# One core, a gMLP and RWKV-7 encoder: the inverse's stores on GpSimd's queue with another order of loads and post-processing, and the low parts of three weight matrices kept in DRAM

## The chip, the cores and the metric

The kernel runs on one core of one Trainium2 chip. The metric is the time of one execution on the device in microseconds. Engines are TensorE (PE; PEld is its loading of weights), VectorE (DVE), ScalarE (ACT), GpSimd (POOL) and SyncE (SP). SP, ACT and POOL can issue DMAs; "SPq", "ACTq" and "POOLq" in the profile are such issues.

## What is computed

An encoder trunk for 1024 tokens of 1024 features, with two residual layers, a SwiGLU FFN after each and a final RMSNorm:

```python
for layer in range(DEPTH):                      # DEPTH = 2
    hn = rms_norm(h, mix_norm[layer])
    if layer % 2 == 0:
        h = h + hybrid_ab_mixer(hn, ...)        # gMLP + pooled means
    else:
        y, v_first = rwkv7_time_mix(hn, ...)
        h = h + y
    h = h + swiglu(rms_norm(h, ffn_norm[layer]), w_gate, w_up, w_down)
return rms_norm(h, final_norm)
```

In the RWKV layer, with xx the shift by one token,

```python
xr, xw, xk, xv, xa, xg = [h + xx * mu[i] for i in range(6)]
r, k, v = xr @ w_r, xk @ w_k, xv @ w_v
# per head, for each token t:
sa = einsum('bhvk,bhk->bhv', state, a_t)
state = state * w_t[:, :, None, :] + sa[..., None] * b_t[:, :, None, :] + v_t[..., None] * k_t[:, :, None, :]
y_t = einsum('bhvk,bhk->bhv', state, r_t)
# then a normalisation per head, a bonus, a gate and @ w_o
```

## The kernel before

**Tiles and halves.** The tokens are worked on in two halves of 512 (h = 0 and 1). Features are 8 tiles of 128. Dense products are float32 by three float32r products: a weight tile of 128x1024 is split into a high part (ACT copies it, L159, "whi", "dhi", "ahi") and a low part (DVE subtracts the high part from the raw tile, L160, "wlo", "dlo", "alo"), and `mm3` (L407 to L411) adds hi·hi, lo·hi and hi·lo.

**Weights.** All weight tiles stand in one list, `plan`, in the order of their use. `load_at` (L123) loads a raw tile by a DMA of ACT's queue, `split_at` splits it, and `take` hands a tile out and keeps two loads and one split ahead. The pool `wst` holds 3 buffers each of raw, high and low tiles.

**Order.** The program is written as generators that are interleaved: `drive(dense, side)` mixes a stream of dense matmuls with side work. A scheduler then orders the instructions of each engine by dependences, priorities and its own estimates; on the chip each engine works through its list in that order, and an instruction that waits holds up all behind it on the same engine.

**Stages.** By the trace: the mixer of layer 0 until about 420 us; its FFN up to 560; the down projection of half 0 from 560 to 740 (`steps_a`, with `wa1` beside it); gates and low-rank factors until 830; `project(0)` from 830 to 1045; `recur(0)` from 1045 to 1250; output projection and norms until 1380; `project(1)` to 1590, `recur(1)` to 1810; the rest of the FFN and the final norm to the end.

**`project(h)`** computes for each pair of heads p = 0 to 7 the products for k and r (weights "k" and "r"), the decays (`cum`, a scan on DVE, L1347), and from them `ar` and `bk`, the scaled operands of the recurrence. Of these, `ar`'s first column (L1374) and the product kkn·av (L1377) are on POOL; L1381 on DVE makes `bk` from the latter, and `late` lets PE multiply `ar` and `bk` (L1257, tile "aux"). SP stores ar and bk to `ab_d`. After p = 3 and p = 7 starts `invert` (L1432 to L1454): 31 steps of two DVE operations (L1443, L1448) invert unit lower triangular 32x32 blocks of four pairs, a copy (L1450) transposes, and three DMAs of SP store the result in `xi_d` (L1452: 64 partitions of 32 rows of 64 numbers; L1454 twice: 64 of 32 rows of 32). These steps lie between the other DVE work: the first inversion beside p = 4 to 7, the second beside the products for v.

**`recur(h)`** works through 8 chunks of 64 tokens. `load(c)` loads ab (L1506), XT (two DMAs from `xi_d`, L1510) and uv (L1513, L1514) by SP. For each chunk come `gram` (bk times ar, then masked into gt, L1530), `flip_bk` (products with the identity), `below` (products with XT) and `burst` (the chain through the state S, uv and the output ysb). All of these matmuls have one line, L1491. Dense matmuls of the FFN are put in between. `stream` (L1842) loads h for them. After two chunks, `post` normalises their output (statistics per head, L1690), in pieces that `between` calls during the next burst; `turn_out` (L1714) transposes and gates it.

Of the kernel before, what the change touches and what calls it, by code (L numbers as in the profile page):

```python
# [16 lines left out]
P = 128  # L17
D = 1024
# [27 lines left out]
def tile_trunk(  # L46
# [79 lines left out]
    def whl():  # L126
        return wst.tile([P, D], F32R, tag="whi", name="whi"), wst.tile([P, D], F32R, tag="wlo", name="wlo")

    def split_at(i):
        if i >= len(plan) or i in ready:  # L130
            return
        load_at(i)
        if i not in raws:
            return
        key, _, view, dest = plan[i]
        if key[0] in makes:
            ready[i] = makes[key[0]](i)
            return
        raw = raws[i]
        to = (dest or whl)()  # L140
        if to is None:
            return
        hi, lo = to
        splits.get(key[0], lambda i, *t: split(*t))(key[1], view(raw), view(hi), view(lo))
        ready[i] = hi, lo

    def take(key):
        i = pos[0]
        assert plan[i][0] == key, (plan[i][0], key)
        pos[0] += 1  # L150
        split_at(i)
        load_at(i + 1)
        if i + 1 in raws:
            load_at(i + 2)
        split_at(i + 1)
        return ready.pop(i)

# [1274 lines left out]
    def invert(h, p0, iat, tmp):  # L1432
# [18 lines left out]
        to = xi_d[h][p0 : p0 + 4].rearrange("p r c q i x -> (p r c) q i x")  # L1451
        sp.dma_start(to[:, 0, :, 0:64], x2[0:64].rearrange("s i a j -> s i (a j)"))  # L1452
        for q in range(2):
            sp.dma_start(to[:, q, :, 64 - 32 * q : 96 - 32 * q], x2[64:128, :, 0, :])  # L1454

# [13 lines left out]
    def recur(h, wp, stream, ratio):  # L1469
# [34 lines left out]
        def load(c):  # L1504
            ab = wt("ar", 2, [P, 2, 8, 2, 64])
            sp.dma_start(ab, ab_d[h][c])  # L1506
            ar, bk = ab[:, 0], ab[:, 1]
            XT = wt("XT", 2, [P, 8, 96])
            for r in range(2):
                sp.dma_start(XT[rows[r]], xi_d[h][:, r ^ (c % 2), c].rearrange("p q i x -> (q i) p x"))  # L1510
            uv = wt("uv", 2, [P, 2, 8, 64])
            vs = v_d[h][c * 64 : c * 64 + 64]
            sp.dma_start(uv[64:128, 0], vs[:, 0])  # L1513
            loaded[0] = sp.dma_start(uv[0:64, 1], vs[:, 1])  # L1514
            gt = wt("gt", 2, [P, 8, 2, P])
            C[c] = (ar, bk, uv, gt, XT)

# [71 lines left out]
        def burst(c, bkt, w1):  # L1589
# [53 lines left out]
            if more:  # L1643
                bkt = flip_bk(c + 1)
                if turned or pieces:
                    for _ in pieces.pop():
                        pass
                    turned.pop()()
# [14 lines left out]

        turned, chain, pieces = [], [None], []

        def between():
            if pieces:
                with tc.issue_after(chain[0]):
                    next(pieces[0], None)

        def post(jj):
            ysb = [ypair.pop(0) for _ in range(2)]
            j = h * 4 + jj
# [13 lines left out]
            yield  # L1687
            for r in range(2):
                for p in range(8):
                    dve.bn_stats(out=st[:, r, p, :], in_=ysb[r][:, p, :])  # L1690
                yield
# [49 lines left out]
        with tc.issue_after(loaded[0].ins):  # L1741
            stream_loaded = stream()
        with tc.issue_after(stream_loaded):
            load(1)
        yield START * ratio
# [8 lines left out]
        for c in range(8):  # L1754
            bkt, w1 = yield from burst(c, bkt, w1)
            yield BURST / 2
            if c % 2 == 1:
                pieces[:] = [post(c // 2)]
                next(pieces[0])
            yield BURST / 2  # L1760
        for _ in pieces[0]:
# [198 lines left out]

    drive(steps_a, wa1())
    hn1 = project_norm(0, np_, norm_bcast(acc[0]))
# [148 lines left out]
```

## Time and profile before

| | us |
|---|---|
| runs | 2401.15, 2406.74, 2410.41 (median 2406.74) |
| profiled execution, device time | 2407.23 |
| its span in the trace | 2405.5 |
| PE busy | 2319.2 |
| DVE busy | 1464.6 |
| ACT busy | 946.9 |
| POOL busy | 171.2 |
| DMA traffic | 347.97 MB, mean 145 GB/s |

The profiled execution is 0.5 us longer than the median of the runs. Its span leaves out 1.7 us around it. A busy time sums the instructions of an engine; "PEclk" is the share of the full TensorE clock that was granted; "DMA share" is the mean busy share of 16 DMA engines. A row of waits gives the waiting engine, tile and line, then what ended the wait, the total, the number of times and the longest. Line numbers are those of the kernel before.

### The profile page before, as it was taken

The page shows a single profiled execution, that of the slowest core. Times are in us where ns is not written, and L with a number is a line of the kernel's source. Part 1 is how long each engine was busy: PE and PEld are TensorE (multiplying, and loading weights), DVE is VectorE, ACT ScalarE, POOL GpSimd, SP SyncE. Part 2 cuts the span into 40 slices and gives each one's busy share as a digit, 9 for nine tenths or more (in the row PEclk, how much of TensorE's full clock was granted, in tenths as well). Part 3 has the DMA queues.
Part 4 walks back from the last instruction along what each step waited for, and adds up shares of the span by engine and source line. Part 5 has one row for each costly group of instructions (what it writes and reads, how often), then busy time and mean ns, then how long its engine had stood idle before and what let it go on. Part 6 is the DMA issues. An engine that isn't in the chain of part 4 may idle for free.

```text
span 2405.5 us, 37578 instructions
## 1 busy us (share of the span) xinstructions
PE 2319.2 (96%) x15315; PEld 1893.9 (79%) x15315; DVE 1464.6 (61%) x2312; ACT 946.9 (39%) x1467; POOL 171.2 (7%) x195
## 2 busy tenths in 40 slices
PE   8999999999999999889899999998999999999998
PEld 6888888888888788667777777777778788888886
DVE  6445775665568858656768958765664546444443
ACT  6233444444224755323336665423332225222223
POOL 0200000000000022101100022101010001000001
PEclk9999999999999999999999999999999999999999
DMA  5114472334765565775445475776534433433231
GB/s 181 53 49 145 149 198 83 129 99 146 283 226 191 156 173 140 209 218 157 130 135 165 148 199 147 193 222 177 163 89 149 123 88 119 127 96 97 79 114 44
DMA packets 446157, 347.97 MB, mean 145 GB/s; under 512 B 119776, under 2 KB 393312, under 8 KB 443680
## 3 DMA queue, kind: packets, MB, share of 16 engines
q10 hardware_dynamic: 266048, 195.33, 27.3%
q1 hardware_dynamic: 179936, 150.25, 20.9%
q8 instruction: 120, 1.97, 0.4%
q14 instruction: 53, 0.43, 0.1%
HBM read 266.47 MB, written 79.04 MB: 144 GB/s over the span
## 4 chain that ended last, share of the span: by engine, by line
PE 77%; DVE 9%; DMA 6%; issue 2%; ACT 2%; SPq 2%; POOL 2%; ACTq 0%; POOLq 0%; DVEq 0%
PE mm L409 17%; PE mm L410 17%; PE mm L411 17%; PE mm L740 5%; PE mm L742 5%; PE mm L741 5%; PE sm L1491 3%; DMA ar<-ab_d 1%; DVE wlo L160 1%; DMA raw<-y_d 1%; SPq L1454 1%; DVE it L1443 1%; DMA raw<-in_ffn_w_down_dram 1%; PE mm L590 1%; PE mm L591 1%
## 5 line engine op out<-in xcount | busy, mean ns | idle before, releaser
L409 PE MATMUL mm<-ahi,whi 128*128 128x512 f32 x1376 | 541.0, 394 | 4.2 <-ACT ahi L159 2.6
L410 PE MATMUL mm<-alo,whi 128*128 128x512 f32 x1376 | 542.0, 394 | 0.9 <-DVE alo L160 0.9
L411 PE MATMUL mm<-ahi,wlo 128*128 128x512 f32 x1376 | 540.6, 393 | 1.6 <-DVE wlo L160 1.6
L159 ACT ACTIVATE whi<-raw 128x1024 fp32r<-128x1024 f32 (+2 forms) x284 | 286.3, 1014 | 507.1 <-PE mm L410 367.7
L160 DVE TENSOR_TENSOR wlo<-raw,whi 128x1024 fp32r<-128x1024 f32 (+2 forms) x284 | 337.6, 1192 | 233.6 <-ACT whi L159 212.4
L409 PEld LDWEIGHTS mm<-ahi,whi 128*128 128x128 f32 x1376 | 259.0, 188 | 62.9 <-issue 3.5
L411 PEld LDWEIGHTS mm<-ahi,wlo 128*128 128x128 f32 x1376 | 259.2, 188 | 58.5 <-DVE wlo L160 2.9
L410 PEld LDWEIGHTS mm<-alo,whi 128*128 128x128 f32 x1376 | 259.3, 188 | 57.4 <-issue 2.9
L503 DVE TENSOR_TENSOR h<-h,mm 128x512 f32<-128x512 f32 x276 | 185.9, 684 | 156.1 <-PE mm L411 152.9
L411 PE MATMUL mm<-hidhi,wdlo 128*128 128x512 f32 x304 | 119.6, 394 | 0.0
L409 PE MATMUL mm<-hidhi,wdhi 128*128 128x512 f32 x304 | 117.2, 392 | 2.3 <-ACT sg L957 2.3
L410 PE MATMUL mm<-hidlo,wdhi 128*128 128x512 f32 x304 | 118.6, 390 | 0.0
L740 PE MATMUL mm<-ahi,whi 128*128 128x512 f32 x296 | 115.6, 390 | 0.0
L741 PE MATMUL mm<-alo,whi 128*128 128x512 f32 x296 | 115.2, 389 | 0.0
L742 PE MATMUL mm<-ahi,wlo 128*128 128x512 f32 x296 | 113.6, 389 | 0.0
L965 DVE TENSOR_TENSOR sg<-sg,mm 128x512 f32<-128x512 f32 x52 | 35.7, 686 | 125.7 <-PE mm L411 125.7
L159 ACT ACTIVATE wdhi<-raw 128x1024 fp32r<-128x1024 f32 x42 | 43.6, 1058 | 169.0 <-PE mm L410 126.9
L160 DVE TENSOR_TENSOR wdlo<-raw,wdhi 128x1024 fp32r<-128x1024 f32 x42 | 51.4, 1223 | 30.9 <-ACT wdhi L159 29.2
L409 PEld LDWEIGHTS mm<-hidhi,wdhi 128*128 128x128 f32 x304 | 57.2, 188 | 14.7 <-ACT sg L957 2.7
L411 PEld LDWEIGHTS mm<-hidhi,wdlo 128*128 128x128 f32 x304 | 57.2, 188 | 12.2 <-issue 0.5
L410 PEld LDWEIGHTS mm<-hidlo,wdhi 128*128 128x128 f32 x304 | 57.2, 188 | 12.0 <-issue 0.2
L409 PE MATMUL mm<-xhi,whi 128*128 128x512 f32 (+1 forms) x160 | 64.9, 406 | 0.0
(392 smaller groups left out, 4226.2 us busy)
## 6 DMA issues: line engine op xcount, KB each, us to landing
raw<-in_ffn_w_down_dram ACTq DMA_DIRECT2D x88, 512.0 KB
raw<-in_ffn_w_gate_dram ACTq DMA_DIRECT2D x74, 512.0 KB
raw<-in_ffn_w_up_dram ACTq DMA_DIRECT2D x74, 512.0 KB
hid_d<-hid SPq DMA_DIRECT2D x36, 512.0 KB
ar<-ab_d SPq DMA_DIRECT2D x16, 1024.0 KB
hd<-hid_d SPq DMA_DIRECT2D x26, 512.0 KB
raw<-in_ab_w_in_dram ACTq DMA_DIRECT2D x16, 512.0 KB
raw<-in_ab_w_out_dram ACTq DMA_DIRECT2D x16, 512.0 KB
```

Of the source, the lines that this page charges most:

```text
L159: act.activation(hi, src, AF.Copy)
L160: (eng or dve).tensor_tensor(out=lo, in0=src, in1=hi.bitcast(F32), op=ALU.subtract)
L409: pe.matmul(o, whi, xhi, start=first, stop=False)
L410: pe.matmul(o, whi, xlo, start=False, stop=False)
L411: newest[0] = pe.matmul(o, wlo, xhi, start=False, stop=last).ins
L503: dve.tensor_tensor(out=H[h][:, m, :], in0=H[h][:, m, :], in1=o, op=ALU.add)
L590: pe.matmul(ops[j], xhi[:, k, sl], whi[:, kk], start=(k == 0), stop=False)
L740: pe.matmul(o, wh[:, k, :], x[0][:, k, :], start=st, stop=False, skip_group_check=True)
L741: pe.matmul(o, wh[:, k, :], x[1][:, k, :], start=False, stop=False, skip_group_check=True)
L742: pe.matmul(o, wl[:, k, :], x[0][:, k, :], start=False, stop=k == 3, skip_group_check=True)
L965: dve.tensor_tensor(out=s, in0=s, in1=o, op=ALU.mult)
L1491: i = f(*args, **kw)
```

## The change

It has two parts.

**Part A, the recurrence's data.** `invert` issues its three stores from GpSimd's queue. `load(c)` loads ab and uv first and XT after them, in a new function `load_x`; for chunk 0, XT is loaded behind the four loads of `stream`, and chunk 1 behind that. The post-processing of two chunks starts ahead of the odd chunk's burst instead of behind it: one piece is let through in an odd burst, any number in an even one, and the output is taken from the list piece by piece.

**Part B, the low parts.** `prepare` runs beside the down projection of half 0, behind `wa1`. For w_r and w_k it works through four units of 1 MB each: a DMA of GpSimd loads the unit, ACT copies the high part and DVE subtracts it (two operations each), and a DMA of GpSimd stores the low part in `rk_d`. In both projections, the low tiles of r and k are loaded from there by SP, two tiles ahead, and only the high part is made. The low tiles of v are made in half 0 as before and stored by SP in `vl_d`, and loaded from there in half 1.

```diff
+    rk_d = dram.tile([2, 4, P, 8, 256], F32, name="rk_d")
+    vl_d = dram.tile([8, P, 8, P], F32, name="vl_d")
+    lows = {}
...
+    def low_at(i):
+        if i >= len(plan) or i in lows:
+            return
+        key = plan[i][0]
+        if low_of(key) is not None and (key[0] != "v" or key[1]):
+            lows[i] = wst.tile([P, D], F32R, tag="wlo", name="wlo")
+            sp.dma_start(v3(lows[i].bitcast(F32)), low_of(key))
...
     def split_at(i):
...
         raw = raws[i]
+        low_at(i)
+        if i in lows:
+            ready[i] = wst.tile([P, D], F32R, tag="whi", name="whi"), lows[i]
+            act.activation(ready[i][0], raw, AF.Copy)
+            return
...
         ready[i] = hi, lo
+        if low_of(key) is not None:
+            sp.dma_start(low_of(key), v3(lo.bitcast(F32)))
...
         dve.tensor_copy(x2[:, :, 0, :], xi.rearrange("p i c -> p c i"))
         to = xi_d[h][p0 : p0 + 4].rearrange("p r c q i x -> (p r c) q i x")
-        sp.dma_start(to[:, 0, :, 0:64], x2[0:64].rearrange("s i a j -> s i (a j)"))
+        pool.dma_start(to[:, 0, :, 0:64], x2[0:64].rearrange("s i a j -> s i (a j)"))
         for q in range(2):
-            sp.dma_start(to[:, q, :, 64 - 32 * q : 96 - 32 * q], x2[64:128, :, 0, :])
+            pool.dma_start(to[:, q, :, 64 - 32 * q : 96 - 32 * q], x2[64:128, :, 0, :])
...
-            XT = wt("XT", 2, [P, 8, 96])
-            for r in range(2):
-                sp.dma_start(XT[rows[r]], xi_d[h][:, r ^ (c % 2), c].rearrange("p q i x -> (q i) p x"))
...
+            if c:
+                load_x(c)
+
+        def load_x(c):
+            for r in range(2):
+                loaded[0] = sp.dma_start(C[c][4][rows[r]], xi_d[h][:, r ^ (c % 2), c].rearrange("p q i x -> (q i) p x"))
...
         with tc.issue_after(stream_loaded):
+            load_x(0)
+        with tc.issue_after(loaded[0].ins):
             load(1)
...
         for c in range(8):
-            bkt, w1 = yield from burst(c, bkt, w1)
-            yield BURST / 2
             if c % 2 == 1:
                 pieces[:] = [post(c // 2)]
                 next(pieces[0])
-            yield BURST / 2
+            open_[0] = (99, 1)[c % 2]
+            bkt, w1 = yield from burst(c, bkt, w1)
+            yield BURST
...
+    def prepare():
+        yield from wa1()
+        for n, w in enumerate((rwkv_w_r[0], rwkv_w_k[0])):
+            for u in range(4):
+                raw, hi = (pr.tile([P, 8, 256], t, tag=g, bufs=2, name=g) for t, g in ((F32, "praw"), (F32R, "phi")))
+                pool.dma_start(raw, w[:, u * 256 : u * 256 + 256].rearrange("(k p) m -> p k m", p=P))
+                for q in (slice(0, 4), slice(4, 8)):
+                    yield 0.8
+                    tc.cur_priority += AHEAD
+                    act.activation(hi[:, q], raw[:, q], AF.Copy)
+                    dve.tensor_tensor(
+                        out=raw[:, q].bitcast(F32R), in0=raw[:, q], in1=hi[:, q].bitcast(F32), op=ALU.subtract
+                    )
+                    tc.cur_priority -= AHEAD
+                pool.dma_start(rk_d[n, u], raw)
...
-    drive(steps_a, wa1())
+    drive(steps_a, prepare())
```

Counted over the program, DVE's subtractions for wlo fall from 254 to 214, and 16 for praw come in; ACT gets 16 copies phi; GpSimd 8 loads and 8 stores of 1 MB and the 12 stores of the inverse; SP 32 loads from rk_d, 8 stores to and 8 loads from vl_d, and loses the 12. The matmuls are the same in number.

The lines of the changed kernel differ: L1374, L1377 and L1437 of before are L1402, L1405 and L1465; L1381 is L1409; L1452 and L1454 are L1480 and L1482; L1425 is L1453; L1506, L1510, L1513 and L1514 are L1534, L1546, L1538 and L1539.

**SP at the start of `recur(1)`.** Before:

```order
L1425 DMA v_d_1977<-epx 256x1x256
L1452 DMA xi_d_1983<-xi 64x32x64
L1454 DMA xi_d_1983<-xi 64x32x32 x2
L1506 DMA ar<-ab_d_1975 128x2048
L1510 DMA XT<-xi_d_1983 64x8x96 x2
L1513 DMA uv<-v_d_1977 64x512
L1514 DMA uv<-v_d_1977 64x512
L1740 DMA S<-state_d 128x512
L1842 DMA h<-h_d_85 128x1024 x4
L1506 DMA ar<-ab_d_1975 128x2048
```

Now:

```order
L1453 DMA v_d_1979<-epx 256x1x256
L1534 DMA ar<-ab_d_1977 128x2048
L1538 DMA uv<-v_d_1979 64x512
L1539 DMA uv<-v_d_1979 64x512
L1771 DMA S<-state_d 128x512
L1875 DMA h<-h_d_87 128x1024 x4
L1546 DMA XT<-xi_d_1985 64x8x96 x2
L1534 DMA ar<-ab_d_1977 128x2048
```

The inverse's stores are gone from SP, the ab load (ar) follows the last store of v, and the load of XT stands behind the loads of h. In `recur(0)` the order is the same, without the load of S.

**GpSimd at p = 7 of `project(0)`.** The names are ar (L1374), kkn (L1377), the exponentials' copy pct and the cleared tile xi of the second inversion. Before:

```order
L1081 TENSOR_SCALAR sg<-sg 128x512
L1081 TENSOR_SCALAR av<-av 128x512
L1353 COPY pct<-epx 128x8
L1374 TENSOR_SCALAR ar<-kkn 128x8
L1377 TENSOR_TENSOR kkn<-kkn,av 128x512
L1437 MEMSET xi 128x2048
```

Now:

```order
L1109 TENSOR_SCALAR sg<-sg 128x512
L1109 TENSOR_SCALAR av<-av 128x512
L1381 COPY pct<-epx 128x8
L1402 TENSOR_SCALAR ar<-kkn 128x8
L1480 DMA xi_d_1984<-xi 64x32x64
L1482 DMA xi_d_1984<-xi 64x32x32 x2
L1405 TENSOR_TENSOR kkn<-kkn,av 128x512
L1465 MEMSET xi 128x2048
```

The first inversion's three stores stand between ar and kkn. In `project(1)` they stand two rows higher, between av and pct.

**DVE from p = 6 to the end of the first inversion of `project(0)`.** it and xi are the inversion's steps, the copy of xi its end, bk (L1381, now L1409) what PE waits for. Before, around bk of p = 7:

```order
L1448 TENSOR_TENSOR xi<-xi,it 128x7x25
L160 TENSOR_TENSOR alo<-raw,ahi 128x1024
L1182 TENSOR_TENSOR xlo<-mix,xhi 128x512
L1189 SCALAR_TENSOR_TENSOR mix<-hn_5530,vec,mix 128x512
L1443 TENSOR_TENSOR it<-iat,xi 128x156
L1381 TENSOR_TENSOR bk<-kkn,em 128x8x64
```

Now, from the last steps of the inversion:

```order
L1476 TENSOR_TENSOR xi<-xi,it 128x31
L188 TENSOR_TENSOR wlo<-raw,whi 128x1024
L1478 COPY xi<-xi 128x32x32
L1210 TENSOR_TENSOR xlo<-mix,xhi 128x512
L188 TENSOR_TENSOR alo<-raw,ahi 128x1024
L1398 SCALAR_TENSOR_TENSOR ar<-kkn,epx 128x8x63
L1210 TENSOR_TENSOR xlo<-mix,xhi 128x512
L1217 SCALAR_TENSOR_TENSOR mix<-hn_5600,vec,mix 128x512 x2
L188 TENSOR_TENSOR alo<-raw,ahi 128x1024
L1210 TENSOR_TENSOR xlo<-mix,xhi 128x512 x2
L1409 TENSOR_TENSOR bk<-kkn,em 128x8x64
```

Before, bk of p = 7 came with six steps of the inversion still to do; now the inversion and its copy are done ahead of it.

More of the change, by code (lines that the diff above doesn't have):

```diff
@@ L127, in whl, with low_of @@
         return wst.tile([P, D], F32R, tag="whi", name="whi"), wst.tile([P, D], F32R, tag="wlo", name="wlo")
+    rk_d = dram.tile([2, 4, P, 8, 256], F32, name="rk_d")
+    vl_d = dram.tile([8, P, 8, P], F32, name="vl_d")
+    lows = {}
+    def low_of(key):
+        if key[0] in ("r", "k"):
+            return rk_d["rk".index(key[0]), key[2] // 2][:, :, key[2] % 2 * P : key[2] % 2 * P + P]
+        return vl_d[key[2] * 4 + key[3]] if key[0] == "v" else None
+    def low_at(i):
[5 more added lines that the diff above has]
+            sp.dma_start(v3(lows[i].bitcast(F32)), low_of(key))
     def split_at(i):
@@ L155, in take @@
         split_at(i + 1)
+        i2 = i + 2
+        if i2 < len(plan) and plan[i2][0][0] in acts:
+            i2 += 1
+        low_at(i2)
         return ready.pop(i)
@@ L1514, in load @@
             loaded[0] = sp.dma_start(uv[0:64, 1], vs[:, 1])
-            gt = wt("gt", 2, [P, 8, 2, P])
-            C[c] = (ar, bk, uv, gt, XT)
+            C[c] = (ar, bk, uv, wt("gt", 2, [P, 8, 2, P]), wt("XT", 2, [P, 8, 96]))
+            if c:
[3 more added lines that the diff above has]
+                loaded[0] = sp.dma_start(C[c][4][rows[r]], xi_d[h][:, r ^ (c % 2), c].rearrange("p q i x -> (q i) p x"))
         def gram(c, q):
@@ L1644, in burst @@
                 bkt = flip_bk(c + 1)
-                if turned or pieces:
-                    for _ in pieces.pop():
-                        pass
+                if c and c % 2 == 0:
+                    exhaust(pieces.pop())
                     turned.pop()()
@@ L1662, in burst @@
             return bkt, w1
-        turned, chain, pieces = [], [None], []
+        turned, chain, pieces, open_ = [], [None], [], [0]
         def between():
-            if pieces:
+            if pieces and open_[0]:
+                open_[0] -= 1
                 with tc.issue_after(chain[0]):
@@ L1671, in post @@
         def post(jj):
-            ysb = [ypair.pop(0) for _ in range(2)]
+            ysb = []
             j = h * 4 + jj
@@ L1688, in post @@
             for r in range(2):
+                ysb.append(ypair.pop(0))
                 for p in range(8):
@@ L1959, in wa1 @@
         scale_wa1()
-    drive(steps_a, wa1())
+    pr, pr_es = open_pool(name="pr", bufs=1, side="right")
+    def prepare():
[14 more added lines that the diff above has]
+    drive(steps_a, prepare())
+    pr_es.close()
     hn1 = project_norm(0, np_, norm_bcast(acc[0]))
```

## The prediction

> **What bounds the kernel now.** I read the page's busy times first, then the busy time by stage, then what the tensor engine (PE) waits for, and last the chains around the longest waits.
>
> ```profile
> span 2405.5 us, 37578 instructions
> PE 2319.2 (96%) x15315; PEld 1893.9 (79%) x15315; DVE 1464.6 (61%) x2312; ACT 946.9 (39%) x1467; POOL 171.2 (7%) x195
> ```
>
> PE is busy for 2319.2 of 2405.5 us, and the change leaves its matmuls as they are. So at most 86.3 us of idle time, and what is lost to a lower clock, can be won. The next view gives five stages: the half-0 down projection, projection and recurrence of half 0, and the same two of half 1. Columns: window, length, then busy time of PE, PEld, DVE, ACT and POOL, the granted PE clock, the DMA share and GB/s.
>
> ```profile
> 560.00:740.00 180.00, 179.31 (x790) 147.71 (x789) 112.95 (x151) 53.81 (x70) 5.11 (x5) 1.00 0.63 226
> 830.00:1045.00 215.00, 201.03 (x1150) 163.16 (x1148) 150.11 (x257) 106.12 (x165) 38.26 (x48) 0.98 0.66 174
> 1045.00:1250.00 205.00, 184.63 (x3095) 148.64 (x3096) 130.83 (x288) 62.56 (x125) 20.18 (x8) 0.95 0.54 158
> 1380.00:1590.00 210.00, 203.10 (x1157) 165.86 (x1156) 151.35 (x258) 107.94 (x166) 38.43 (x47) 0.98 0.67 179
> 1590.00:1810.00 220.00, 206.13 (x3172) 166.51 (x3170) 132.21 (x286) 69.86 (x132) 20.19 (x8) 0.98 0.58 162
> ```
>
> The down projection has 0.7 us of idle PE: it can only lose. The other four hold 14.0, 20.4, 6.9 and 13.9, together 55 us. What ended those waits, as total, times and longest:
>
> ```profile
> PE sm L1491 <- DMA ar<-ab_d: 12.8, 3, 9.5
> PE aux L1257 <- DVE bk L1381: 7.3, 5, 2.0
> PE sm L1491 <- ACT uv L1611: 5.5, 4, 2.4
> PE sm L1491 <- DVE ysb L1714: 4.5, 5, 1.2
> PE bo L1287 <- DVE k L1386: 1.8, 1, 1.8
> PE aux L1416 <- DVE wlo L160: 1.4, 1, 1.4
> ```
>
> The first row is the start of the recurrences. The chain there (start, length, what) shows why the load is late:
>
> ```profile
> 1036.50 0.61 SPq L1452
> 1037.16 2.63 SPq L1454
> 1039.84 4.50 SPq L1454
> 1044.43 7.93 DMA ar<-ab_d
> ```
>
> SyncE (SP) issues the three stores of the inverse until 1044.34, and only then the first load of ab, for which PE waits until 1052.4.
>
> **Starts of the recurrences.** In the new SP order the ab load follows the last store of v; the inverse's stores are on GpSimd (POOL).
>
> ```profile
> 1017.73 0.84 SPq L1425 DMA_DIRECT2D v_d<-epx  x1
> 1048.93 1.27 SPq L1510 DMA_DIRECT2D XT<-xi_d  x2
> 1051.56 2.12 SPq L1842 DMA_DIRECT2D h<-h_d  x4
> ```
>
> So the load can go at about 1019, 25 us sooner, and lands long before PE needs it at 1042.9: the 9.5 us go. In half 1 the wait is one of 2.7:
>
> ```profile
> PE sm L1491 <- DMA ar<-ab_d: 2.7, 1, 2.7
> 1585.53 0.61 SPq L1452 DMA_DIRECT2D xi_d<-xi  x1
> 1586.19 6.17 SPq L1454 DMA_DIRECT2D xi_d<-xi  x2
> ```
>
> After such waits the clock is half for a while (same columns as above):
>
> ```profile
> 862.40:869.20 6.80, 6.12 (x18) 5.18 (x19) 4.86 (x7) 3.42 (x6) 2.19 (x3) 0.50 0.77 184
> 1046.70:1056.90 10.20, 4.49 (x68) 4.16 (x69) 2.04 (x4) 0.00 (x0) 0.00 (x0) 0.50 0.97 280
> 1603.10:1606.50 3.40, 3.40 (x47) 2.88 (x40) 1.29 (x2) 0.00 (x0) 0.00 (x0) 0.50 1.05 318
> ```
>
> Half of 4.49 and of 3.40, 2.2 and 1.7, is lost there. Gain at both starts: 9.5 + 2.2 + 2.7 + 1.7 = 16.1 us. What is late next is XT, which still needs the inverse: it is loaded behind the stores and the four loads of h. Call T the time in which GpSimd puts out the three stores. The inverse is ready at 1036.5; T, some 2 us of landing, about 3.5 for h and XT on SP and 2 to 3 of transfer give 1044.5 + T. PE reaches the first product with XT after the grams, 8 flips and 12 dense matmuls, about 1048.5. So XT costs nothing up to T = 4, and T − 4 per recurrence beyond it.
>
> The page "DMA: Bandwidth & Descriptors" of the Trainium skill, section "Issuing engines are not separate DMA queues", says that another queue saves only the sequencer's time to initiate a transfer, usually little. Here that time is 7.7 us of SP (1036.50 to 1044.34); by this rule the first term would be those 7.7 and not 9.5, but the trace shows the load itself free to start 25 us sooner.
>
> **The stores on GpSimd.** No DMA of GpSimd is in the trace of before, so T has to be bounded. Below: three issues like SP's of L1452, 3 × 0.61 = 1.8. Above: the slowest triple on SP, 0.62 + 11.28 = 11.9:
>
> ```profile
> 979.23 0.62 SPq L1452 DMA_DIRECT2D xi_d<-xi  x1
> 979.89 11.28 SPq L1454 DMA_DIRECT2D xi_d<-xi  x2
> ```
>
> I take T = 4, nearer the lower end: the L1452 store has as many rows as each of the others and took 0.61, so the longer entries look like waiting for a full queue. T matters because of what stands behind the first inversion's stores on GpSimd: the last key product of the projection, for which DVE's bk and then PE wait. The rows of p=7 in half 0, and two of half 1:
>
> ```profile
> 961.89 4.16 POOL L1374 TENSOR_SCALAR ar<-kkn 128x8 f32<-128x8 f32 x1 [3.20 <-ACT kkn L1369]
> 966.14 1.83 POOL L1377 TENSOR_TENSOR kkn<-kkn,av 128x512 f32<-128x512 f32 x1
> 968.75 0.69 PE L1257 MATMUL aux<-ar,bk 64*64 64x64 f32 x32 [2.01 <-DVE bk L1381]
> 1505.55 1.67 DVE L1347 TENSOR_TENSOR_SCAN cum<-smask,sg 128x256 f32<-128x256 f32 x2 [0.51 <-POOL sg L1081]
> 1511.35 4.17 POOL L1374 TENSOR_SCALAR ar<-kkn 128x8 f32<-128x8 f32 x1 [3.20 <-ACT kkn L1369]
> ```
>
> PE already waits 2.0 us there. In half 0 the stores now stand between the two GpSimd operations, and by the new DVE order the inverse is complete at about 964, so kkn and PE slip by T (or by about 2.5 if T is less, because DVE now does the end of the inversion ahead of bk). In half 1 they stand ahead of the whole group; the inverse is complete right behind cum, at about 1508.3, and GpSimd was idle until 1511.35, so the slip is T − 3. With T = 4: 4 + 1, and 2 us for the clock after the longer wait, estimated from the 2.2 above. Cost 7.
>
> **Low parts of r and k, and of v in half 1.** Each projection loses 16 of DVE's subtractions, half 1 another 8; the mean is 1.19 us:
>
> ```profile
> L160 DVE TENSOR_TENSOR wlo<-raw,whi 128x1024 fp32r<-128x1024 f32 (+2 forms) x284 | 337.6, 1192 | 233.6 <-ACT whi L159 212.4
> ```
>
> That is 19 and 29 us of DVE's 150. PE gains only where it waited for DVE: bk 7.3 less the two p=7 waits of 2.0, k 1.8, wlo 1.4, and half of the 6.12 at half clock near 862: 9.5 us. The low parts now come by DMA, 8 and 12 MB into stages whose share is 0.66; at 0.66 per 174 GB/s, 59 GB/s adds 0.22, so it still fits but each load is slower. I take 6 of 9.5, bounds 0 and 9.5.
>
> **The preparation in the down stage.** It adds 16.8 MB to the 40.7 (226 GB/s × 180 us), 16 copies to ACT, 16 subtractions to DVE, 16 DMAs to GpSimd. DVE and ACT have room (113 and 54 of 180 busy). DMA:
>
> ```profile
> 620.00:640.00 20.00, 20.00 (x89) 16.06 (x88) 14.50 (x19) 3.77 (x4) 0.00 (x0) 1.00 1.02 385
> 690.00:700.00 10.00, 10.00 (x45) 8.28 (x45) 5.08 (x7) 2.01 (x2) 0.00 (x0) 1.00 0.23 73
> 700.46 0.33 ACTq L123 DMA_DIRECT2D raw<-in_ffn_w_down_dram  x1
> 705.83 1.06 ACT L159 ACTIVATE dhi<-raw 128x1024 fp32r<-128x1024 f32 x1 [7.44 <-DMA raw<-in_ffn_w_down_dram]
> ```
>
> 57.5 MB at 385 GB/s take 149 of 180 us, so the total fits. But a weight tile issued at 700.46 lands at 705.8, its split follows, and PE uses it from 708.6: about a microsecond of slack once both halves are made. A load slowed by a third costs some 2 us. I take 5 for two or three such tiles, bounds 0 and 30 (seven tiles at 4 to 5).
>
> **Post-processing.** Spreading it takes DVE and ACT work out of the bursts whose uv and ysb PE waits for, 5.5 + 4.5 = 10.0 us in both recurrences. Chunk for chunk the work is the same, so I take 4; bounds −3 (new crowding in even bursts) and 10.
>
> **Sum.** Gains 16.1 + 6 + 4 = 26.1, costs 7 + 5 = 12: −14 us. The profiled execution took 2407.23 (span 2405.5), 0.5 above the median 2406.74 of the runs. Forecast 2393 us. A difference of 0.5%, 12 us, is about what a measurement of this kernel can tell from none.
>
> **Rivals.** *Slower: GpSimd's stores hold up the projection.* At T = 11.9 PE slips 11.9 and 8.9, XT is late by 7.9 twice, and about 8 goes to the clock: 45 instead of 7, so +24: 2431 us. From T = 7 the change gains nothing, from about 9.5 it is slower by 12. For it: GpSimd's own entries can be long for little work, as the 4.17 us for a product of 128x8 shows; against: the 0.61 of L1452. Chance 0.14. The Trainium skill, page "SBUF — State Buffer", box on the "DVE blocks DMA" trap, says that DVE copies between SBUF tiles keep GpSimd from writing descriptors, and gives 3.1 us for a transfer of 0.62 alone; by that T would be 9.3 where copies run, and the time about 2417; here DVE runs mostly two-input products then, so no run shows it yet.
>
> *No change.* T near 7, or DVE's relief and post-processing worth nothing (−14 + 10 = −4): 2403 to 2407. For it: much of DVE's time is off PE's path in a kernel with PE at 96%. Chance 0.21.
>
> *Down stage starves.* Weight tiles late in seven groups, 30 instead of 5: +11, 2418 us. For it: the slices at 1.02 share; against: the slice at 0.23. Chance 0.10.
>
> *More is freed.* T = 1.8 (cost 2.5), the full 9.5 on DVE, 2 in the down stage: −25, 2382 us. Chance 0.17.
>
> *The change not doing what it says* has little room: the order of the instructions shows the moved stores, the loads and the missing subtractions.
>
> **Numbers.** Forecast case 0.38, from 2386 to 2401, of which 0.28 lies over 12 us below the median. Faster: 0.28 + 0.17 = 0.45. Same: 0.10 + 0.21 = 0.31. Slower: 0.14 + 0.10 = 0.24. The likeliest sign holds less than half, so the range takes both sides: from 2374 (the freed case, 2382, less the 6 by which the post-processing term can exceed my value and the 2 of the down stage) to 2431.
>
> **What would show it.** Right: no wait for ab_d at the first grams and full clock at 1046 and 1603; GpSimd's three stores within about 4 us; PE's wait for bk at p=7 near 6 us in half 0 and 3 in half 1; below 5 us idle in the down stage; fewer waits for bk, k and wlo. Wrong: XT in place of ab; the stores taking 8 us or more; waits for dhi, dlo or ahi between 620 and 740; waits for wlo by DMA in the projections.

## The result, and the profile after

The changed kernel is slower: 2436.65 us (median of 4 runs, 2430.03 to 2441.04) against 2406.76 for the kernel before on the same chip, a ratio of 1.0136 with a 95% interval of 1.0115 to 1.0157. The forecast was 2393 us. The head of the profile after, of the execution of 2430.03 us:

```profile
span 2428.3 us, 37651 instructions
PE 2325.7 (96%) x15315; PEld 1895.0 (78%) x15315; DVE 1435.5 (59%) x2288; ACT 963.1 (40%) x1483; POOL 188.0 (8%) x223
```

DVE has 29 us less to do, as meant. PE's idle time, span less busy, grew from 86.3 to 102.6, and its busy time by 6.5 for the same matmuls; the mean granted clock of the execution fell from 0.986 to 0.982. The same stages as in the prediction, with the same columns:

```profile
560.00:740.00 180.00, 158.02 (x672) 127.92 (x671) 108.00 (x139) 57.25 (x71) 16.33 (x21) 0.95 0.76 279
830.00:1045.00 215.00, 201.96 (x1152) 163.58 (x1151) 137.27 (x242) 117.16 (x185) 41.51 (x54) 0.98 0.82 232
1045.00:1250.00 205.00, 192.30 (x3143) 154.39 (x3142) 133.23 (x285) 66.89 (x125) 20.22 (x11) 0.98 0.60 168
1380.00:1590.00 210.00, 197.97 (x1119) 160.94 (x1119) 124.38 (x229) 106.63 (x166) 38.51 (x54) 0.96 0.85 236
1590.00:1810.00 220.00, 211.57 (x3173) 170.01 (x3172) 134.72 (x273) 74.17 (x133) 19.72 (x10) 0.98 0.62 175
```

The down stage, the one that could only lose, went from 0.7 to 22.0 us of idle PE. The windows are fixed in time while the work moves through them, so a mark in the work is better than a window. The first product with xhi ends the down stage and what belongs to it; its rows before and after (start, length, line, operation):

```profile
799.17 0.39 PE L409 MATMUL mm<-xhi,whi 128*128 128x512 f32 x1
```

```profile
825.22 0.39 PE L437 MATMUL mm<-xhi,whi 128*128 128x512 f32 x1
```

It comes 26.1 us later. Up to this mark PE runs the same number of matmuls in all the kernels with part B's preparation that are compared below, so the nth matmul can be set against the nth: the one at 640.2 before starts 7.6 us late, the one at 690.1 starts 24.7 late, the one at 750.2 starts 26.0 late. So some 8 us are lost before 640, and some 18 behind two waits that end at 692 and 708, with the clock at half from 700.6 to 710.8.

The longest waits of PE after the change, over the whole span:

```profile
PE mm L437 <- ACT dhi L187: 15.0, 2, 12.3
PE aux L1285 <- DVE bk L1409: 10.7, 4, 6.2
PE mm L437 <- DVE h L531: 7.2, 5, 3.8
PE mm L437 <- ACT ahi L187: 5.1, 3, 2.9
PE mm L437 <- DVE h L952: 4.7, 1, 4.7
```

The wait for ab is gone from the list. The last row, 4.7 us for h, is where the first 8 us are lost. DVE's rows of this addition before and after, and PE's row after (start, length, what, then the idle time and what ended it):

```profile
621.87 1.28 DVE L924 TENSOR_TENSOR h<-ahi,mm 128x512 f32<-128x512 f32 x2 [3.05 <-DMA hid_d<-hid]
625.88 1.28 DVE L952 TENSOR_TENSOR h<-ahi,mm 128x512 f32<-128x512 f32 x2 [7.83 <-DMA hid_d<-hid]
626.62 0.80 PE L437 MATMUL mm<-ahi 128*128 128x512 f32 x1 [4.66 <-DVE h L952]
```

DVE waits for the store of the FFN's hidden activations (hid_d), which ends 4 us later than before, and PE waits for DVE. The granted clock is 0.50 from 625.6 to 632.4. PE does not wait for a weight tile here.

The first row of the list, dhi, is the larger part of the down stage's loss. The rows of the chain ahead of the 12.3 us (start, length, what):

```profile
680.97 0.09 POOL rk_d L2010
681.54 1.18 POOL wa L1120
682.79 2.06 POOL wa L1120 x2
684.92 1.05 POOL wa L1120
685.99 7.62 DMA wa_d<-wa
693.73 11.88 DMA raw<-in_ffn_w_down_dram
706.00 1.04 ACT phi L2005
707.03 0.95 ACT dhi L187
```

A store of the preparation is issued on GpSimd, then the four products wa that scale the decay's weights, then their store, and only then does the load of a down-projection tile go out, lands after 11.88 us, is split, and PE goes on at 708.03. The load has nothing to do with wa in the computation. But wa's two tiles are taken from the pool of raw weight tiles, which has three buffers; until wa is stored, one buffer is left. Before, the four products ran from 656.3 to 661.5; now the loads of wa go out at 664.2 and not at 647.1, the products stand behind the preparation's stores, and they run from 681.5 to 686. Traffic adds to this wait: the tile took 11.88 us to land, where the one of 700.46 in the prediction's rows was there in 5.4.

GpSimd's stores of the inverse cost what the forecast took, and hold up the last product of the projection:

```profile
993.19 1.21 POOL L1480 DMA_DIRECT2D xi_d<-xi  x1
994.41 2.18 POOL L1482 DMA_DIRECT2D xi_d<-xi  x2
1000.17 1.13 PE L1285 MATMUL aux<-ar,bk 64*64 64x64 f32 x32 [6.24 <-DVE bk L1409]
```

T is 3.4 us, and PE's wait at p = 7 rose from 2.0 to 6.2. In half 1, where the prediction had 3, PE does not wait for bk at p = 7 (its products start at 1543.41).

The start of the first recurrence shows what is late in place of ab:

```profile
1045.96 0.33 SPq L1534 DMA_DIRECT2D ar<-ab_d  x1
1071.99 1.95 SPq L1875 DMA_DIRECT2D h<-h_d  x4
1075.61 1.29 DVE L531 TENSOR_TENSOR h<-h,mm 128x512 f32<-128x512 f32 x2 [6.94 <-DMA h<-h_d]
1076.35 0.80 PE L437 MATMUL mm<-hidhi,whi 128*128 128x512 f32 x1 [3.82 <-DVE h L531]
```

The load of ab is issued 25 us ahead of the first gram, and PE does not wait for it. The loads of h, which stand behind it on SP, wait until the inverse's stores on GpSimd have landed (the first of them has these DMAs among its waits, and goes 8.0 us after GpSimd's last issue ended at 1063.98). DVE's residual addition waits for h and PE for DVE: 3.8 us are given back within a few microseconds of the gain, and behind this wait the clock is half again, as it was behind the wait for ab (columns of the stage tables):

```profile
1076.10:1082.90 6.80, 4.87 (x15) 3.88 (x16) 3.88 (x7) 1.20 (x2) 0.00 (x0) 0.50 1.07 297
```

### The profile page after: what moved, and what is told of

It reads as the page before. It is cut to its first block, busy times and chain, and to the rows that moved or that the text cites. A ratio compares the mean times of both kernels' runs of the same rounds, so it can differ in the third digit from the quotient of the medians.

```text
span 2428.3 us, 37651 instructions
## 1 busy us (share of the span) xinstructions
PE 2325.7 (96%) x15315; PEld 1895.0 (78%) x15315; DVE 1435.5 (59%) x2288; ACT 963.1 (40%) x1483; POOL 188.0 (8%) x223
## 4 chain that ended last, share of the span: by engine, by line
PE 77%; DMA 8%; DVE 8%; issue 3%; ACT 2%; POOL 1%; SPq 1%; ACTq 0%; POOLq 0%; DVEq 0%
PE mm L437 17%; PE mm L438 17%; PE mm L439 17%; PE mm L768 5%; PE mm L770 5%; PE mm L769 5%; PE sm L1519 4%; DMA raw<-in_ffn_w_down_dram 1%; DMA raw<-y_d 1%; DVE xi L1476 1%; DVE it L1471 1%; DMA praw<-in_rwkv_w_r_dram 1%; DMA ab_d<-ar 1%; PE yp L1519 1%; PE mm L618 1%
## 5 line engine op out<-in xcount | busy, mean ns | idle before, releaser
L187 ACT ACTIVATE whi<-raw 128x1024 fp32r<-128x1024 f32 (+2 forms) x244 | 244.1, 1008 | 461.6 <-PE mm L438 358.7
L188 DVE TENSOR_TENSOR wlo<-raw,whi 128x1024 fp32r<-128x1024 f32 (+2 forms) x244 | 286.3, 1178 | 198.3 <-ACT whi L187 189.8
L437 PE MATMUL mm<-hd,dhi 128*128 128x512 f32 x160 | 64.2, 401 | 17.6 <-ACT dhi L187 15.0
L437 PEld LDWEIGHTS mm<-hidhi,wdhi 128*128 128x128 f32 x304 | 57.1, 188 | 14.5 <-ACT sg L985 2.2
L439 PEld LDWEIGHTS mm<-hidhi,wdlo 128*128 128x128 f32 x304 | 57.0, 188 | 12.5 <-issue 0.7
L438 PEld LDWEIGHTS mm<-hidlo,wdhi 128*128 128x128 f32 x304 | 57.1, 188 | 11.9 <-issue 0.2
```

Of the source, the lines that this page charges most:

```text
L187: act.activation(hi, src, AF.Copy)
L188: (eng or dve).tensor_tensor(out=lo, in0=src, in1=hi.bitcast(F32), op=ALU.subtract)
L437: pe.matmul(o, whi, xhi, start=first, stop=False)
L438: pe.matmul(o, whi, xlo, start=False, stop=False)
L439: newest[0] = pe.matmul(o, wlo, xhi, start=False, stop=last).ins
```

## Experiments

Every kernel was timed beside the kernel before on its own chip, where that one's median lay between 2400.2 and 2401.7; ratios, not microseconds, are compared with the result above. The expectations state totals on the scale of the forecast's runs (2407), unless they name a difference.

**The two parts by themselves.** Part A is the hunks on invert, load, post and the order of bursts; part B those on low parts and prepare.

> Part A alone: the inverse's stores on GpSimd, the new order of loads, the earlier post-processing; low parts as before, nothing prepared in the down stage. Theory 1 (all of the loss is made in the down stage by part B's preparation): idle there back to under 1 us, the first gram's wait gone (13 us), about 5 us more at p = 7 of half 0: 2394 to 2402 us. Rival (what the start of the recurrences wins is given back elsewhere, the stores on GpSimd cost as much): 2405 to 2412 us.

> Part B alone: low parts prepared and kept, the inverse's stores on SP, loads and post-processing as before. Theory 1: the down stage loses about 26 us as in the changed kernel, the wait for ab at the first gram is back, DVE's relief gives 0 to 6: 2427 to 2435 us. Rival (part A shares the blame): 2408 to 2418 us.

A alone: 2414.72 us, ratio 1.005 (1.0031 to 1.0068). B alone: 2442.41 us, 1.0172 (1.0149 to 1.0194). B makes the loss in the down stage: it ends at 825.4, as in the changed kernel, and in A alone at 798.9, as before. But A alone is a loss too, against theory 1; at 14.5 us it is more than the 5 that its rival allowed. B alone loses more than both parts together (the two intervals just overlap) and more than the 28 us of theory 1. PE's wait for ab at the first gram, 9.4 us, is back in it, as theory 1 has it. In A alone the wait for ab is gone; the row that replaced it in PE's list:

```profile
PE sm L1491 <- ACT uv L1613: 17.1, 8, 4.9
```

It was 5.5 in four waits. The rows around one of the eight (DVE's and ACT's, then PE's):

```profile
1101.64 0.17 DVE L1706 SCALAR_TENSOR_TENSOR mean<-mean,var 128x16 f32<-128x16 f32 x1 [1.86 <-POOL var L414]
```

```profile
1101.85 2.76 ACT L1709 ACTIVATE ysb<-ysb,mean,var 128x64 f32<-128x64 f32 x8 [5.58 <-DVE mean L1706]
1104.51 0.57 ACT L1613 ACTIVATE uv<-sm 64x512 f32<-64x512 f32 x1
```

```profile
1105.14 0.47 PE L1491 MATMUL sm<-uv,bkt 128*64 128x64 f32 x2 [3.09 <-ACT uv L1613]
```

ACT's eight copies of the earlier post-processing stand ahead of uv and wait for the statistics; uv, which PE needs for the next state, stands behind them. Two runs divide A:

```diff
 # e7_a_nopost: stores on GpSimd, order of loads; not: pieces, open_, ysb.append
 # e8_post:     pieces, open_, ysb.append; not: stores, order of loads
```

> Part A without the earlier post-processing: the inverse's stores on GpSimd and the new order of loads only. Theory 2 (in part A alone the earlier post-processing puts its eight ACT copies ahead of uv, and this eats the gain at the starts): waits for uv back near 5 us from 17, the first gram's wait gone, some 4 us given back where a dense product waits for h: 6 to 14 us below the kernel before. Rival (the stores on GpSimd or the order of loads cost by themselves): as part A alone, 8 to 16 us above it.

> The earlier post-processing alone; stores, loads and low parts as before. Theory 2: waits for uv rise from 5 to 15 us or more, the 9.5 us wait for ab stays: 8 to 18 us above the kernel before. Rival: within 5 us of it.

Stores and loads: 2401.37 us, 0.9998 (0.9981 to 1.0015). Post-processing: 2414.33 us, 1.0055 (1.0039 to 1.0072). So the earlier post-processing costs 13 us by itself, all that A costs; in its trace the waits for uv (8.4) and for Q (4.2) grew, together by some 7 us. That is less than the 15 that theory 2 wanted for uv, and the rest of the 13 is not placed. In the changed kernel, whose lists differ again, the waits for uv are only 2.4 us, so how much of these 13 us is in its loss is open, as is why B alone loses more than both parts together. And the moved stores and loads gain nothing, against the 6 to 14 expected, and lose nothing, against the 8 to 16 of the rival.

**Where the gain of the starts went.** In the run without the earlier post-processing, the norm behind the first recurrence has this first row of waits, in the window 1220 to 1290:

```profile
PE mm L409 <- ACT ahi L159: 9.1, 1, 9.1
```

It was 2.6. (The execution of this trace took 2407.1 us, one of the longer ones of this run.) PE's order tells more: between the first gram and the last transpose of that recurrence stand 468 dense matmuls, 402 before. They are missing as cover behind the recurrence. One reading is that the scheduler draws them forward because XT comes later in SP's order. Theory 3 says that the gain is given back behind the recurrence. In the changed kernel itself it is 441, and its longest wait for ahi is 2.9 us, so there this loss is smaller.

```diff
 # e10_queue: only this
-        sp.dma_start(to[:, 0, :, 0:64], x2[0:64].rearrange("s i a j -> s i (a j)"))
+        pool.dma_start(to[:, 0, :, 0:64], x2[0:64].rearrange("s i a j -> s i (a j)"))
...
 # e9_loads: only load_x and its calls, the stores on SP
...
 # e13_hold, e14_hold34 (36 and 34 steps): as e7_a_nopost, and
-    drive(ffn(0, 1, nxt["hn"], f, D0P[3:], nd=2))
-    drive(steps_b)
+    rest = ffn(0, 1, nxt["hn"], f, D0P[3:], nd=2)
+    for _ in range(36):
+        next(rest)
+    with tc.issue_after(tail[0]):       # the last transpose of recur(0)
+        drive(rest)
+        drive(steps_b)
```

> The inverse's stores on GpSimd and nothing else; SP loads ab, XT and uv in the old order. Theory 3 (what the starts win is given back behind the recurrence, because dense matmuls are drawn forward as cover: 468 instead of 402 stand in the first recurrence): the first gram waits no longer for ab, but the norm behind the recurrence waits 8 us or more for its operand, total within 5 us of the kernel before. Rival (the order of loads spoils it): 6 us or more below it.

> The new order of loads alone, with the inverse's stores on SP, where they still stand ahead of the load of ab. Theory: the first load of ab still waits for SP, so the wait of 9 us at the first gram stays: within 4 us of the kernel before. Rival (the order of loads and not the queue is what removes the wait): 6 us or more below it.

> Stores on GpSimd and the new order of loads, and the last dense products of the stage (from the down part of the fourth group of the FFN on) are queued on PE behind the first recurrence's last transpose, so that 414 dense matmuls instead of 468 stand in the recurrence (402 before). Theory 3: the wait for ahi behind the recurrence falls from 9 to 3 us or less, the gain of the start remains: 5 to 12 us below the kernel before. Rival (PE then waits in the recurrence for its chain instead): within 4 us of it.

> As the held-back kernel with 12 dense matmuls more held back (402 stand in the first recurrence, as before). The order of the second recurrence changes with it (521 dense matmuls there instead of 459). Theory 3: 4 to 12 us below the kernel before. Rival (which order the scheduler finds in the second recurrence decides as much as what is moved on purpose): 5 us or more away from the held-back kernel, in either direction.

The queue alone: 2405.74 us, 1.0024 (1.0009 to 1.004), with a wait for ahi of 8.8: as theory 3 has it. But a part is given back at the start already. XT, whose load waits for the stores to land, stands on SP ahead of h there, and behind the first gram PE waits for h:

```profile
1046.14 0.79 PE L409 MATMUL mm<-hidhi,whi 128*128 128x512 f32 x1 [5.59 <-DVE h L503]
```

And 468 dense matmuls stand in the recurrence of this run too, with XT at its old place in SP's order; so that place is not needed for it, and why the scheduler draws them forward stays open. The loads alone: 2414.01 us, 1.006 (1.004 to 1.008); the wait for ab stays (8.9), as expected, but the 14 us of loss were not expected by either side, and what makes them is not shown. Here 453 dense matmuls stand in the recurrence. Held back to 414: 2412.57 us, 1.0045 (1.0026 to 1.0065); to 402: 2397.92 us, 0.9992 (0.9975 to 1.0009). Holding back did what it should at its place: no wait for ahi above 3 us is left. But PE now waits at the end of the recurrence, here in the run with 402, window 1190 to 1290:

```profile
PE sm L1493 <- DVE ysb L1718: 9.5, 2, 8.4
```

So theory 3 holds for where the idle time shows, and its expected gains of 5 to 12 and 4 to 12 us did not come: one kernel lost 11 us, more than its rival's 4 too, and the other is level with before. It looks as if the chain of recurrence and norm takes its time with cover or without it, and PE waits for it at the one place or the other. The two held kernels differ by 12 dense matmuls in the first recurrence and by 14.7 us in their medians; the scheduler also filled the second recurrence with 521 instead of 459. Which order it finds weighs as much as what is moved on purpose.

**How far a trace stands for its kernel.**

> The kernel before once more, unchanged, for a second trace. Theory: the down stage ends within 1 us of the first trace; from the projections on, where tiny DMAs and waits decide, stages differ by some us from one execution to the next, with the same order of instructions. Rival: all stages agree within 1 us, so that differences of 5 us between traces are effects of the edits.

2399.04 us, 0.9997 (0.9986 to 1.0007). The first product with xhi starts at 799.6, 0.4 from the first trace. Then the traces part: from p = 0 to p = 7 of the first projection 106.0 against 109.1 us, the first gram 5.8 sooner (1046.6 against 1052.4), and the span is 2395.4 against 2405.5, all with the same instructions in the same order. So the theory holds: the down stage can be read from one trace to within a microsecond, a later stage to within some three to six, and of the sum over the later stages only the ratios speak.

**What the down stage loses.**

```diff
 # e4_ownwa
-        raw = [wst.tile([P, D], F32, tag="raw", name="wa1") for _ in range(2)]
+        raw = [pr.tile([P, D], F32, tag="wa1", bufs=2, name="wa1") for _ in range(2)]
 # e5_traffic: as e4, with no act.activation and no dve.tensor_tensor in prepare
 # e12_half: as e4, for w_r only (k's low parts are then made as before)
-        for n, w in enumerate((rwkv_w_r[0], rwkv_w_k[0])):
+        for n, w in enumerate((rwkv_w_r[0],)):
 # e15_delay: as e4, and
+                with tc.issue_after(scaled[0]):     # the last product wa on GpSimd
                     pool.dma_start(raw, ...)
```

> The changed kernel with one thing undone: the two tiles in which the decay's weights wa are scaled have buffers of their own and no longer occupy two of the three raw buffers of the weight stream (the copies phi rotate through half-size tiles to make room). Traffic and preparation are the same. Theory 1a (the scaling stands behind the preparation's stores on GpSimd and holds the raw buffers, so the next weight load goes out late): the 12 us wait for dhi goes, down stage loses under 10 instead of 26 us, total 2412 to 2421 us. Rival 1b (the DMA engines are full, each load lands late) or 1c (ACT stands at phi for its load): 2430 us or more, waits for dhi and ahi as before.

> As the changed kernel with buffers of their own for wa (the earlier run), but the preparation only loads and stores its units: it makes no high parts and subtracts nothing, so that what it stores are whole weights and not low parts (the products with them are left wrong). What stays is the traffic. Theory 1b (what is left of the down stage's loss is traffic): the down stage loses as much as with the copies and subtractions, 8 to 15 us against before, total within 4 us of the earlier run (16 to 21 above the kernel before). Rival 1c (it is the copies on ACT and the subtractions on DVE, which wait for their loads): down stage within 4 us of before, 8 us or more below the earlier run.

> As the changed kernel with buffers of their own for wa, but only w_r is prepared (half the traffic of the preparation); k's low parts are made by DVE in both projections. Theory 1b (what is left of the down stage's loss is DMA traffic): the down stage loses about half of the 15 us that it lost with all of it, 5 to 9, total 6 to 12 us below that run. Rival (the preparation's mere presence, its order on ACT and GpSimd): down stage loses 12 or more.

> As the changed kernel with buffers of their own for wa; besides, the preparation's loads are queued on GpSimd behind the scaling of wa, so that the first two loads of 1 MB leave some 15 us later, at about 630 to 640 and not at 614. Traffic in sum is the same. Theory 1d (what is left of the down stage's loss is made by the first two loads, which meet the transfers that already fill the DMA engines from 618 to 640): the down stage loses 0 to 6 us against before instead of 15. Rival 1b (the sum of the traffic): 11 us or more.

With buffers of its own for wa: 2422.02 us, 1.0072 (1.0047 to 1.0098), so about 15 us of the 33 that 1.0136 stands for are gone. The waits for dhi are gone from the down stage, and the first product with xhi comes at 814.5 instead of 825.2. Theory 1a is right for 10.7 us there; of the 26.1, 15.4 are left, not under 10. Matmul by matmul it took away more: the 18 us at 692 and 708 are gone whole, and at 760 this run is only 9.7 late. The rest of the 15.4 is a new wait at the end of the stage, which the changed kernel does not have:

```profile
778.59 0.80 PE L437 MATMUL mm<-hd,dhi 128*128 128x512 f32 x1 [4.51 <-DVE h L531]
```

Traffic alone, without copies and subtractions: 2457.08 us, 1.0232 (1.021 to 1.0253), the mark at 821.2. Nothing slows the units down now, and all eight go through by 705. Its busy times while they do, in the columns of the stage tables:

```profile
620.00:640.00 20.00, 10.99 (x34) 7.64 (x32) 5.89 (x7) 0.37 (x1) 5.39 (x7) 0.82 1.02 413
640.00:660.00 20.00, 16.47 (x59) 12.94 (x60) 10.06 (x14) 3.06 (x3) 2.04 (x3) 0.76 1.02 401
660.00:680.00 20.00, 20.00 (x90) 16.57 (x89) 10.04 (x13) 3.16 (x4) 2.03 (x3) 1.00 1.03 397
```

PE loses 12.5 us up to 660, though ACT and DVE do none of the preparation: 1c is not needed for it. The 22 us at the mark are more than the 8 to 15 of theory 1b, since the units now follow each other faster. What PE waits for is again the hidden activations: 4.9 us for h as above, and 6.9 us in three waits for their loads (hd from hid_d), not a weight tile. (The rest of that run's 55 us is in later stages, waits for uv of 23.9 us among them, under another order.) But half the units lose as much in the down stage as all of them, mark at 813.9, against 1b as a sum over the stage and as the rival has it: 2429.32 us, 1.0112 (1.0087 to 1.0136). What that run loses in the down stage is lost before 660. Its rows there (DVE, then PE):

```profile
636.80 3.64 DVE L2007 TENSOR_TENSOR praw<-praw,phi 128x1024 fp32r<-128x1024 f32 x2 [5.81 <-ACT phi L2006]
641.09 0.79 PE L437 MATMUL mm<-hd,dhi 128*128 128x512 f32 x1 [6.01 <-DVE h L531]
```

Besides the 4.0 us for h by the late store, PE waits 6.0 us because the preparation's subtraction stands ahead of the residual additions on DVE; it waits for phi, and phi stands on ACT behind three loads of weight tiles (issued at 634.2, before at 625.5). With all units and wa's own buffers the same wait is 2.5 us. So the order on ACT and DVE has a share, and half the units are no clean test of the traffic. Both runs point at the first two loads of 1 MB: they come at about 614, ahead of the stretch from 620 to 640 in which the engines were full before, too.

The delay confirms this for the first part: the group of down products that starts at 626.9 before, and at 632.3 with wa's own buffers alone, starts at 628.3, and the matmul of 640.2 is 2.4 us late and not 9.4. (The delay moves the copies and subtractions with the loads, so it does not divide the two.) Yet the mark moves only to 811.6, and the total is 2425.99 us, 1.0112 (1.0095 to 1.0129), because a wait at the end of the stage took its place:

```profile
775.14 0.79 PE L437 MATMUL mm<-hd,dhi 128*128 128x512 f32 x1 [7.05 <-DVE h L531]
```

DVE's list there has the norm's steps and splits (hn, alo, mix) from 761 to 774, and the residual addition h behind them, which PE needs to go on; before, four such additions stood among these steps and PE waited 1.0. In the runs whose preparation ends on DVE at 733 or sooner this wait is about 1 us, in those where it ends at 743 to 752 it is 4.5 and 7.1; that it is the preparation which pushes the additions back is likely, and no run shows it alone. So theory 1d is right for what it named, and wrong that nothing would follow.

**Is part B worth anything?**

> Part A, and the low parts of r, k and v all made by DVE in half 0, stored by SP and loaded in half 1: no preparation in the down stage, 12 MB more written in half 0 and read in half 1. Theory 1: as part A alone, within 4 us, since half 1's DVE relief is worth little to PE: 2393 to 2403 us. Rival (loading low parts by DMA in the projections costs by itself): 6 us or more above part A alone, with waits for wlo by DMA.

> The changed kernel without its three found costs: the post-processing as before, buffers of their own for wa, the preparation's loads behind the scaling of wa. What stays: stores on GpSimd, the new order of loads, all low parts of r and k and half 1's of v from DRAM. Theory 4 (fewer subtractions on DVE are worth nothing to PE, the stores as much as nothing): the down stage within 6 us of before, total within 8 us of it. Rival (DVE's relief is worth 6 us or more once the costs are gone): 5 us or more below it.

```diff
 # e3_reuse: part A and, without prepare, for r, k and v
-        if low_of(key) is not None and (key[0] != "v" or key[1]):
+        if low_of(key) is not None and key[1]:
 # e17_fixed: the changed kernel less the post-processing's order, with e4 and e15
```

Low parts kept from half 0 for half 1: 2428.91 us, 1.012 (1.0089 to 1.0151), 14 us above part A alone, so the rival; but not by waits for wlo (1.3 us). Its largest wait is at the first recurrence, 12.7 us for gt, and behind it stands again h:

```profile
1062.57 1.75 SPq L1874 DMA_DIRECT2D h<-h_d  x4
```

The second inversion ended at 1050 there, 4 us ahead of the first gram (in part A alone it was 10), the stores on GpSimd followed, and h waited for them. The changed kernel less its three found costs: 2427.48 us, 1.0116 (1.0094 to 1.0138). The down stage loses 13 us where 6 were the most expected, and the total misses its 8 us by far; theory 4's other half holds, no gain of part B shows. In part B alone PE's waits for bk and k in the first projection are 3.0 and 1.2 us, before they were 3.3 and 1.8; that is all of DVE's relief that a trace shows there. Why this last kernel loses some 15 us more behind the down stage than stores and loads without B is not settled: 468 dense matmuls stand in its first recurrence too, and its wait for ahi behind it is 9.6 us, but no run took that away alone.

## Why the prediction was wrong

The time rose by 30 us where 14 of gain were forecast. In the two traces the end of the down stage comes 26.1 us later and the end of the span 22.8, so the stages behind it are 3.3 us shorter; by the medians they would be 4 longer. Two executions of one kernel differ by that much, and neither is the 19 us of gain (26.1 less 7) that the forecast had there.

The step that failed most is that on the down stage, put at 5 us with bounds 0 and 30: it measured 26. The term was mis-sized, and its mechanism, weight tiles slowed by traffic that have about a microsecond of slack, is not what the runs show. Some 8 us came from traffic, but by another path: the store of the hidden activations landed 4 us later, DVE's addition waited for it, and PE for DVE. The larger part, 18 us, came from a queue that the step did not follow: the preparation's stores stand on GpSimd ahead of wa's products, whose tiles occupy two of three raw buffers, so that a weight tile's load was issued late; with buffers of their own this part is gone. The step counted GpSimd's 16 new DMAs and named none of the instructions behind them. 57.5 MB in 149 of 180 us was the wrong test as well: it averages over the 20 us in which the engines were full already, and the first two loads met those.

The second failed step is the post-processing, taken as a gain of 4 with bounds −3 and 10. It is a loss of 13 us by itself. "Takes DVE and ACT work out of the bursts" was true only of the even ones; the odd burst got the work, in front of uv. This accounts for about half of the 13 in the trace of that run; in the changed kernel it is not seen at uv.

Third, the starts. The wait for ab was read rightly from the rows, and it is gone at both starts; XT cost nothing at T = 3.4, as worked out. But "what is late next" was asked only of XT. h was next (3.8 us). At the second start the stretch at half clock is gone (the granted clock is 1.00 from 1600 to 1640); at the first, 6.8 us at half clock stand behind the wait for h. With stores and loads alone, cover was lost besides: 66 dense matmuls more stood in the recurrence and left the norm bare (9.1 us; in the changed kernel they are 39 and the longest wait 2.9). The order that was shown to be fuller with dense matmuls there was taken as a help and never counted as a debt. With stores and loads alone the kernel is as fast as before.

Fourth, DVE's relief, 6 of 9.5: no run shows a gain from it. In the changed kernel the waits that it should shorten are longer, 10.7 us for bk (6.2 of them behind the stores) and 3.4 for k, and waits for low tiles by DMA came in, 2.3 and 0.5 us.

Right were the absence of a wait for ab and XT, and in half 0 the slip at p = 7 (4 forecast, 4.2 measured); in half 1, where 1 was forecast, the wait went away. T (4 taken, 3.4 measured) was a choice between 1.8 and 11.9 without a DMA of GpSimd to read from, so its closeness is in part luck. The weighing of the Trainium skill's box on the "DVE blocks DMA" trap ("SBUF — State Buffer") held: the entries of 1.1 to 1.2 us are far from 3.1, beside a DVE that ran two-input products; no copy of DVE ran beside these entries, so what the box says of copies is not tested here. By the rule of the Trainium skill's page "DMA: Bandwidth & Descriptors", section "Issuing engines are not separate DMA queues", the first term would have been 7.7 us and not 9.5. The trace does not bear that out, since the load of ab was issued 25 us ahead of the first gram and the wait for it is gone whole. That the queue alone still gave nothing comes from the waits behind it. Of the rivals, "down stage starves" had the place and 0.10; its 2418 us left out the raw buffers and the post-processing.

## What to carry to other kernels

Before work is added to an engine's queue, list what stands behind it there and which buffers those instructions hold; a buffer pool that a side task borrows from turns a late side task into a late main load. Ask of extra traffic not only which loads it slows but which stores, and who waits for them. Where PE is 96% busy, a wait that is removed is worth only what the next chain leaves: ask which cover was spent on it, and what stands uncovered afterwards. A stage with full DMA engines for 20 us does not average over its 180, so start extra transfers by the slices, not by the stage.

## What the runs showed of the hardware

The three inverse stores took 1.14 to 1.21 us and 1.09 to 1.11 us each as entries on GpSimd, in all four places alike, where on SP a pair of the latter took 6.2 to 11.3 us (four pairs of before); but they landed 6.3 to 12.1 us after their issue. A load of 1 MB on GpSimd took 0.9 to 1.1 us to issue, a store 0.54 to 0.57. And the spread between executions was not expected: the kernel before lay between 2394 and 2410 us over its runs, with one order of instructions, so that differences of 0.2% needed ten runs.
